# PSUM banks dealt anew in one layer of a hybrid encoder: two for projections, three for attention's scores

## The chip, the cores and the metric

The kernel runs on one core of a Trainium2 chip. The metric is the device time of one execution in microseconds (us). The median of three runs before the change is 2429.84 us (2428.33 to 2432.44).

## What is computed

One layer over 2048 prompt tokens and 64 sample tokens of width 1024, in fp32. A combined input projection feeds three mixers: a convolution with a gated linear recurrence (A), a multi-scale pooling (B) and stick-breaking attention with four heads of 64 (C). An output projection and a SwiGLU feed-forward part of width 2816 follow, each with a residual addition.

```python
def trunk_layer(x, lw, conv_buf, lru_h, pool_buf, k_past, v_past, pos0):
    h = rms_norm(x, lw["attn_norm"])
    proj = jnp.einsum("bld,de->ble", h, lw["w_in"])
    x_a, g_a, u_b, q, k, v = jnp.split(proj, SPLITS, axis=-1)
    xc, new_conv = causal_conv(x_a, conv_buf, lw["conv_w"], lw["conv_b"])
    y_lru, new_h = rg_lru(xc, lru_h, ...)
    y_a = y_lru * jax.nn.gelu(g_a, approximate=True)
    y_b, new_pool = multiscale_pool(u_b, pool_buf, pos0, lw["pool_w"], lw["pool_scale"])
    q = rms_norm(q.reshape(B, L, N_HEADS_C, HEAD_DIM), lw["q_norm"]) * (HEAD_DIM ** -0.5)
    k = rms_norm(k.reshape(B, L, N_HEADS_C, HEAD_DIM), lw["k_norm"])
    o = stick_breaking(q, k, v)      # exp(z - sum of softplus(z) over later keys), times v
    x = x + jnp.einsum("ble,ed->bld", jnp.concatenate([y_a, y_b, o]), lw["w_out"])
    h2 = rms_norm(x, lw["ffn_norm"])
    return x + (jax.nn.silu(h2 @ lw["w_gate"]) * (h2 @ lw["w_up"])) @ lw["w_down"]
```

## The kernel before

Every product is made in three matmuls (`mm3`): each operand is split into a rounded high part and a rest, and high x high, high x rest and rest x high are added up in one PSUM bank. A projection of 1024 inputs is therefore a group of 8 x 3 = 24 matmuls.

The prompt is worked in four token groups of 512 (`g` = 0 to 3); group 0 carries the 64 sample tokens along. For each group the input projections come in blocks of 128 outputs (`inproj`): A and G are the input of the recurrence and its GeLU gate, R the recurrence with its two gate products (`ps_g`, one matmul each), B and b the pooling, Q, K and V attention's inputs. Since a bank holds 512 columns, group 0's 576 tokens take two chunks of 288 (`chunks`), the others one of 512. After a Q or K projection the sums of squares of each head are made by matmuls with a selector (`ev_`), for the norm.

Attention goes over query tiles of 128 against up to 512 keys (`att_qtile`): scores in a bank z, a sigmoid by ScalarE in place, a running product (scan) by VectorE from z into `C` in SBUF, then transposes by TensorE into a bank `tp`, a split of these by ScalarE and VectorE, and products with V into the bank `av`. Then come the output projection in chunks of 256 tokens (`OUT`), whose groups are added to the residual on VectorE (L1005), the second norm, and the feed-forward part with a PSUM pool of its own.

PSUM has eight banks; until the feed-forward part they are dealt out by tag. Before: `mm` three (projections, gates, sums of squares from group 1 on, V, output projection), `tp` two, z two, `av` one. A tag's tiles go round its banks: a tile may be written when the last reader of an earlier tile in that bank is done.

```python
    def ps_mm():
        return psum.tile([P, 512], F32, name="mm", tag="mm", bufs=prm("nmm", 3))
    def ps_st(k):
        if k == 0:
            return ps_mm()
...
        if k == 2:
            return psum.tile([P, GW], F32, name="z", tag="z", bufs=prm("nz", 2))
```

The order of the work on each engine is not the program's: a planner with a timeline of its own takes at each step the ready instruction of highest priority, with the banks in view; attention has a priority of its own (`att`). The engines then work these orders strictly in turn. All numbers that steer it stand in the table `PRM`.

Of the kernel before, what the change touches and what calls it, by code (L numbers as in the profile page):

```python
# [2 lines left out]
PRM = {'accf': 2.0, 'aend': 0.0, 'alag': 15.0, 'alag0': 20.0, 'aspan': 4.0, 'att': 100.0, 'b_C': 5.0, 'b_K': 2.0, 'b_V': 2.0, 'b_aTh': 2.0, 'b_aTl': 2.0, 'b_hl': 1.0, 'b_ms': 2.0, 'b_om': 2.0, 'b_raw': 3.0, 'b_rbk': 1.0, 'b_vT': 1.0, 'b_vf': 3.0, 'b_vp': 2.0, 'b_vs': 2.0, 'b_x2': 2.0, 'b_xh': 3.0, 'b_xk': 3.0, 'b_xr': 3.0, 'b_xt': 2.0, 'cpos': 0.0, 'db': 1.0, 'ev': 0.0, 'fine': 1.0, 'ge': 0.0, 'gelb': 2.0, 'h2p': 3.0, 'lru': 100.0, 'md': 2.0, 'mhp': 0.0, 'mlast': 6.0, 'nmm': 3.0, 'nt': 100.0, 'o0': 'P0_P1_p0_G0_m0_A0_L0_R0_p1_S_l0_m1_B0_n0_A1_L1_l1_G1_R1_n1_b0_B1_A2_G2_G3_A3_R2_b1_X_Q0_Q1_R3_q0_u0_K0_q1_K1_u1_k0_k1_V_w0_w1', 'o1': 'A0_G0_A1_R0_G1_S_A2_R1_B0_G2_A3_R2_G3_B1_X_Q0_b0_R3_Q1_K0_q0_q1_u0_V_u1_K1_k0_w0_b1_k1_w1', 'o3': 'A0_G0_A1_R0_B0_G1_A2_R1_b0_G2_R2_G3_B1_A3_b1_R3', 'qlo': 1.0, 'sqb': 1.0, 'stt': 0.0, 'stt0': 2.0, 'vl': 1.0, 'vpp': 0.0, 'wd0': 1.0, 'wd1': 2.0, 'wl': 300.0, 'wm': 0.0, 'wod': 6.0, 'wok': 4.0, 'wsp': 100.0, 'xpl': 6.0, 'xrp': 0.0}  # L3
def prm(n,d):
    return type(d)(PRM.get(n,d))
# [44 lines left out]
def hybrid_layer(ctx: ExitStack, tc: tile.TileContext, x_all, x_t, w_in, w_out, w_gu, w_dn, par, gates, poolw,  # L50
# [29 lines left out]
    def mm3(out, lh, ll, rh, rl, start, stop):  # L80
        mm(out, lh, rh, start, False)
        mm(out, lh, rl, False, False)
        mm(out, ll, rh, False, stop)
# [65 lines left out]
# [6 lines that stand above are left out]
        if k == 1:  # L155
            return ps_t().rearrange('p a b -> p (a b)')
        if k == 2:
            return psum.tile([P, GW], F32, name="z", tag="z", bufs=prm("nz", 2))
        return psum.tile([P, GW], F32, name="av", tag="av", bufs=1)
# [4 lines left out]
    def ps_t():  # L164
        return psum.tile([P, 4, P], F32, name="tp", tag="tp", bufs=prm("ntp", 2))
# [48 lines left out]
    def wsplit(src, spec, on_dve=0, key=None, **ax):  # L214
        w2 = wtile()
        hi, lo = w2[:, 0, :], w2[:, 1, :]
        if key in wkept:
            with hp('wl'):
                sp.dma_start(w2.bitcast(F32), wkept[key])
        else:  # L220
            st = stage()
            with hp('wl'):
                sp.dma_start(st, src)
            with hp('wsp'):
                act.copy(hi, st)
                if on_dve:
                    dve.tensor_tensor(lo, st, hi, ALU.subtract)
                else:
                    rest(lo, hi, st)
            if key is not None:  # L230
                wkept[key] = dram.tile([P, 2, 1024], F32, name=f"wk{key[0]}_{key[1]}")
                sp.dma_start(wkept[key], w2.bitcast(F32))
        return hi.rearrange(spec, **ax), lo.rearrange(spec, **ax)
# [92 lines left out]
    def QK_parts(g, which, j):  # L326
# [3 lines left out]
        def mm_():  # L330
            raw = pq.tile([P, WM], F32, name="raw", bufs=prm("b_raw", 2))
            sq = pq.tile([P, WM], F32, name="sq", bufs=prm("b_sq", 1))
            for ps, a, b in inproj(g, which, j):
                leave(raw[:, a:b], ps[:, :b - a], g, a)
                act.activation(sq[:, a:b], raw[:, a:b] if g == 0 else ps[:, :b - a], AF.Square)
            st["raw"], st["sq"] = raw, sq
# [129 lines left out]
    def chunks(g):  # L466
        return [(0, 288), (288, 576)] if g == 0 else [(0, 512)]
# [3 lines left out]
    def inproj(g, wi, part):  # L471
        hi, lo = hT[g]
        wcnt[0] += 1
        wh, wl = wsplit(w_in[wi, :, part * 1024:(part + 1) * 1024], "p (k e) -> p k e", k=8,
                        on_dve=prm('wd0', 0) <= wcnt[0] < prm('wd1', 0), key=(wi, part))
        res = []
        for (a, b) in chunks(g):
            ps = ps_mm()
            for k in range(KD):
                mm3(ps[:, :b - a], wh[:, k, :], wl[:, k, :], hi[:, k, a:b], lo[:, k, a:b], k == 0, k == KD - 1)  # L480
            res.append((ps, a, b))
        return res
# [296 lines left out]
    def IN(g):  # L779
# [8 lines left out]
        o = "o0" if g == 0 else "o3" if g == NG - 1 else "o1"  # L788
        o = PRM[o].replace("_", " ")
        for tok in o.split():  # L790
# [121 lines left out]
    alag = prm("alag", 0.0)  # L912
# [464 lines left out]
```

## Time and profile before

| | |
|---|---|
| median of three runs | 2429.84 us |
| the profiled execution: its own time | 2430.59 us |
| its span | 2428.8 us |
| TensorE (PE) busy | 2315.6 us, 95% |
| VectorE (DVE) busy | 1561.7 us, 64% |
| GpSimd (POOL) busy | 1112.7 us, 46% |
| ScalarE (ACT) busy | 965.6 us, 40% |
| mean granted clock of TensorE | 0.975 of full speed |

A share of busy time is a mean over stages with different limits. The input projections and attention take the time to about 850 us, the output projection goes on until about 990 us, and the feed-forward part takes the rest. Waits are told as "engine, tile, line <- engine, tile, line that released it". A busy TensorE at a granted clock under 1 is busy for longer with the same work.

### The profile page before, as it was taken

The numbers are of one execution on the slowest core, as the hardware profiler recorded it, in microseconds if no ns is written. First come the engines' busy times: TensorE is split into PE (matmuls) and PEld (weight loads), VectorE is DVE, ScalarE is ACT, GpSimd is POOL, SyncE is SP. The second block draws the span as 40 slices with busy tenths as digits, with TensorE's granted clock in tenths as the row PEclk, the third lists the DMA queues.
The fourth block names the chain that finished last, engine by engine and source line by source line (L and its number), as shares of the span: only waits on it lengthen the run. The fifth ranks groups of instructions, "written<-read, shape, count | busy, mean of one in ns | idle before, by whom it ended". The sixth has DMA issues, their size and how long they took to land.

```text
span 2428.8 us, 38577 instructions
## 1 busy us (share of the span) xinstructions
PE 2315.6 (95%) x14230; PEld 2204.5 (91%) x14230; DVE 1561.7 (64%) x2514; ACT 965.6 (40%) x1804; POOL 1112.7 (46%) x818
## 2 busy tenths in 40 slices
PE   6987999999889989889999999999999999999999
PEld 6976778779678989889999999999999999999999
DVE  4568486796798644696676768655554655555455
ACT  4545364464565422233333343334333433333332
POOL 4533030131131133576565666656565765655552
PEclk8999999999999999999999999999999999999999
DMA  8986777656546354774343348633333563333332
GB/s 281 262 280 197 222 219 225 192 192 206 170 150 175 104 146 129 250 233 131 113 139 118 123 147 267 237 105 122 109 108 114 160 214 108 118 112 108 115 110 74
DMA packets 228478, 399.90 MB, mean 165 GB/s; under 512 B 37697, under 2 KB 99714, under 8 KB 220354
## 3 DMA queue, kind: packets, MB, share of 16 engines
q1 hardware_dynamic: 228290, 397.44, 52.6%
q8 instruction: 112, 1.84, 0.3%
q14 instruction: 76, 0.62, 0.1%
HBM read 300.81 MB, written 96.54 MB: 164 GB/s over the span
## 4 chain that ended last, share of the span: by engine, by line
PE 72%; DVE 12%; DMA 9%; issue 3%; ACT 2%; SPq 1%; POOL 1%; DVEq 0%; ACTq 0%; POOLq 0%
PE gu L78 33%; PE dn L78 20%; PE mm L78 14%; PE z L78 2%; PE av L78 2%; DVE C L661 1%; PE tp L705 1%; DMA rb<-xrow 1%; DMA kscr<-hl 1%; PE tp L78 1%; DVE xc L533 1%; DMA rbk<-row 1%; DMA x1all<-xr 1%; DMA wk<-w 1%; DVE al L1226 1%
## 5 line engine op out<-in xcount | busy, mean ns | idle before, releaser
L86 POOL TENSOR_TENSOR w<-x,w 128x512 fp32r<-128x512 f32 x462 | 640.7, 1401 | 509.7 <-ACT w L1103 478.4
L78 PE MATMUL dn<-ah,wd 128*128 128x352 f32 x2112 | 548.0, 324 | 5.4 <-ACT ah L1225 3.4
L78 PE MATMUL gu<-ht,w 128*128 128x352 f32 x2112 | 545.8, 323 | 7.3 <-DVE u L1180 7.1
L1103 ACT CAST w<-x 128x512 fp32r<-128x512 f32 x462 | 279.0, 619 | 521.2 <-PE gu L78 295.8
L78 PE MATMUL mm<-hTh,w 128*128 128x512 f32 (+3 forms) x1632 | 431.2, 342 | 13.7 <-DVE xr L1005 7.3
L78 PE MATMUL gu<-hb,w 128*128 128x352 f32 x1584 | 417.3, 325 | 9.0 <-DMA x<-in_w_gu 7.3
L1256 DVE TENSOR_TENSOR acc<-dn,acc 128x352 f32<-128x352 f32 x528 | 273.1, 522 | 217.5 <-PE dn L78 216.9
L78 PEld LDWEIGHTS dn<-ah,wd 128*128 128x128 f32 x2112 | 376.4, 189 | 7.6 <-ACT ah L1225 4.2
L78 PEld LDWEIGHTS gu<-ht,w 128*128 128x128 f32 x2112 | 375.1, 188 | 8.9 <-issue 5.9
L78 PE MATMUL dn<-al,wd 128*128 128x352 f32 x1056 | 342.4, 324 | 3.3 <-DVE al L1226 3.3
L78 PE MATMUL gu<-lt,w 128*128 128x352 f32 x1056 | 341.0, 323 | 0.0
L78 PEld LDWEIGHTS mm<-hTh,w 128*128 128x128 f32 x1632 | 290.2, 194 | 44.3 <-DVE xr L1005 8.5
L78 PEld LDWEIGHTS gu<-hb,w 128*128 128x128 f32 x1584 | 284.1, 189 | 11.1 <-ACT w L1103 9.5
L78 PE MATMUL mm<-hTl,w 128*128 128x512 f32 (+3 forms) x816 | 277.6, 341 | 0.8 <-DVE hTl L303 0.4
L78 PE MATMUL gu<-lb,w 128*128 128x352 f32 x792 | 257.1, 325 | 0.0
L86 POOL TENSOR_TENSOR wd<-x,wd 128x512 fp32r<-128x512 f32 x132 | 192.4, 1478 | 51.6 <-ACT wd L1244 51.6
L78 PEld LDWEIGHTS dn<-al,wd 128*128 128x128 f32 x1056 | 199.7, 189 | 4.5 <-DVE al L1226 4.5
L78 PEld LDWEIGHTS gu<-lt,w 128*128 128x128 f32 x1056 | 198.6, 188 | 0.0
L78 PEld LDWEIGHTS mm<-hTl,w 128*128 128x128 f32 x816 | 157.8, 193 | 15.7 <-issue 1.4
L661 DVE TENSOR_TENSOR_SCAN C<-z,C,zero 128x512 f32<-128x512 f32 (+4 forms) x148 | 160.6, 1087 | 13.9 <-ACT z L653 7.5
L1180 DVE TENSOR_TENSOR u<-gu,u 128x352 f32<-128x352 f32 x132 | 68.9, 522 | 129.1 <-PE gu L78 128.8
L78 PEld LDWEIGHTS gu<-lb,w 128*128 128x128 f32 x792 | 150.0, 189 | 0.0
(272 smaller groups left out, 3540.5 us busy)
## 6 DMA issues: line engine op xcount, KB each, us to landing
x<-in_w_gu SPq DMA_DIRECT2D x220, 256.0 KB, 3.3
w<-wk SPq DMA_DIRECT2D x46, 1024.0 KB, 5.7
x<-wsc SPq DMA_DIRECT2D x176, 256.0 KB, 3.4
x<-in_w_dn SPq DMA_DIRECT2D x132, 256.0 KB, 2.8
wsc<-x SPq DMA_DIRECT2D x88, 256.0 KB, 2.7
wk<-w SPq DMA_DIRECT2D x16, 1024.0 KB, 9.1
V<-vscr SPq DMA_DIRECT2D x40, 256.0 KB, 3.8
K<-kscr SPq DMA_DIRECT2D x40, 256.0 KB, 3.6
```

What stands on the lines that cost most here:

```text
L78: pe.matmul(out, lhsT, rhs, start=start, stop=stop)
L86: gp.tensor_tensor(out, src, hi, ALU.subtract)
L533: dve.scalar_tensor_tensor(xc[:, a:b], xa[:, s + j:s + j + b - a], pv("cw", c * 4 + j), xc[:, a:b], ALU.mult, ALU.add)
L661: dve.tensor_tensor_scan(C[:n, :w][:, ::-1], om[:n, :w][:, ::-1], zero1[:n].to_broadcast([n, w]), carry, ALU.mult, ALU.add)
L705: pe.transpose(tp[:, kt, :], at[:, kt * P:(kt + 1) * P], ident)
L1103: act.copy(w[:, 0, :], src)
L1180: add = lambda o, x, y: dve.tensor_tensor(o, x, y, ALU.add)
L1226: dve.tensor_tensor(al[:, cs], o, ah[:, cs], ALU.subtract)
L1256: dve.tensor_tensor(acc[:, d, a:b], ps[:, :HT], acc[:, d, a:b], ALU.add)
```

## The change

In `PRM`, `nmm` goes from 3 to 2, a new entry `nz` of 3 takes the place of the default 2, and `stt` goes from 0 to 2; `stt0` was 2 already. So `mm` has two banks and z three. `ev_` takes its bank from `ps_st(prm('stt0', 0) if g == 0 else prm('stt', 0))`: the sums of squares of groups 1 to 3 move from `mm` to z, where those of group 0 were. In `inproj`, every chunk that does not begin at column 0 takes a bank of z. Only group 0 has such a chunk: columns 288 to 575, that is 224 prompt tokens and the 64 sample tokens.

```diff
-PRM = {... 'nmm': 3.0, 'nt': 100.0, ... 'stt': 0.0, 'stt0': 2.0, ...}
+PRM = {... 'nmm': 2.0, 'nz': 3.0, 'nt': 100.0, ... 'stt': 2.0, 'stt0': 2.0, ...}
...
         for (a, b) in chunks(g):
-            ps = ps_mm()
+            ps = ps_st(2) if a else ps_mm()
             for k in range(KD):
                 mm3(ps[:, :b - a], wh[:, k, :], wl[:, k, :], hi[:, k, a:b], lo[:, k, a:b], k == 0, k == KD - 1)
             res.append((ps, a, b))
```

The planner then writes another order. Three places follow; the numbers in the names tell tiles apart, and the same number is the same tile before and after.

TensorE's order at the first Q projections of group 0: mm_674 and mm_699 (z_699 after) are the two chunks of one projection, mm_755 begins the next, and the tiles tp_475, tp_490 and tp_505 belong to V. Before:

```order
L78 MATMUL mm_674<-hTh_200,w2_667 128x288
L426 MATMUL tp_490<-ident_147,vf_487 128x128 x2
L78 MATMUL tp_475<-vf_472,dm_202 128x256
L78 MATMUL tp_475<-vf_458,em_203 128x256
L426 MATMUL tp_505<-ident_147,vf_502 128x128 x2
L78 MATMUL mm_699<-hTh_200,w2_667 128x288
```

After:

```order
L78 MATMUL z_699<-hTl_201,w2_667 128x288
L78 MATMUL z_699<-hTh_200,w2_667 128x288
L78 MATMUL tp_475<-vf_472,dm_202 128x256
L78 MATMUL tp_475<-vf_458,em_203 128x256
L426 MATMUL tp_505<-ident_147,vf_502 128x128 x2
L78 MATMUL mm_755<-hTh_200,w2_748 128x288
```

The 24 matmuls of the second chunk stand ahead of V's tiles instead of behind them, and the next projection follows these.

TensorE's order in attention of group 3: z_N are the scores of a query tile, C_(N+4) their scan, tp its transposes. The tiles' order is z_6385, 6398, 6421, 6434, 6493, 6506, 6529, 6542. Before:

```order
L78 MATMUL z_6529<-K_6487,q2_6167 128x512 x2
L78 MATMUL mm_7820<-hTh_200,w2_7785 128x256
L78 MATMUL mm_7820<-hTl_201,w2_7785 128x256
L78 MATMUL mm_7847<-hTh_200,w2_7785 128x256
L78 MATMUL mm_7847<-hTl_201,w2_7785 128x256
L78 MATMUL mm_7895<-hTh_200,w2_7785 128x256
L78 MATMUL mm_7895<-hTl_201,w2_7785 128x256
L705 MATMUL tp_6499<-ident_147,C_6497 128x128 x4
L78 MATMUL av_6174<-aTh_6419,V_6381 128x256
L78 MATMUL z_6542<-K_6487,q2_6167 128x512 x2
```

After:

```order
L78 MATMUL z_6529<-K_6487,q2_6167 128x512 x2
L78 MATMUL av_6174<-aTh_6343,V_6305 128x256
L705 MATMUL tp_6391<-ident_147,C_6389 128x128 x4
L78 MATMUL z_6542<-K_6487,q2_6167 128x512 x2
L705 MATMUL tp_6404<-ident_147,C_6402 128x128 x4
```

Behind z_6529 came the transposes of the tile two back (z_6493); now come those of the tile six back (z_6385).

TensorE's order at the gates of group 0's third block: mm_1881 to mm_1890 are the two gate products in two chunks, mm_1913 and mm_1916 the pooling product. Before:

```order
L78 MATMUL mm_1881<-xc_1578,gw_179 128x288
L78 MATMUL mm_1884<-xc_1578,gw_179 128x288
L705 MATMUL tp_1743<-ident_147,C_1741 128x128
L78 MATMUL z_1839<-K_1730,q2_1727 128x384 x2
L78 MATMUL mm_1887<-xc_1578,gw_179 128x288
L78 MATMUL mm_1890<-xc_1578,gw_179 128x288
L705 MATMUL tp_1754<-ident_147,C_1751 128x128 x2
L78 MATMUL z_1852<-K_1730,q2_1727 128x512 x2
L78 MATMUL mm_1913<-xc_1508,pw_180 128x288
L78 MATMUL mm_1916<-xc_1508,pw_180 128x288
```

After:

```order
L78 MATMUL mm_1881<-xc_1578,gw_179 128x288
L78 MATMUL mm_1884<-xc_1578,gw_179 128x288
L78 MATMUL mm_1887<-xc_1578,gw_179 128x288
L78 MATMUL mm_1890<-xc_1578,gw_179 128x288
L78 MATMUL mm_1913<-xc_1508,pw_180 128x288
L78 MATMUL mm_1916<-xc_1508,pw_180 128x288
```

Attention's rows have moved from between the six groups to behind them.

## Rows read from the trace of the kernel before

**Rows 1.** Stretches of 100 us: columns as in the first line.

```profile
core 0: us, PE busy (x) PEld busy (x) DVE busy (x) ACT busy (x) POOL busy (x), PEclk, DMA share, GB/s
...
200.00:300.00 100.00, 90.60 (x465) 76.47 (x465) 57.88 (x116) 40.62 (x80) 20.76 (x10) 0.93 0.74 219
...
700.00:800.00 100.00, 93.46 (x684) 85.64 (x683) 88.40 (x125) 60.23 (x111) 19.16 (x16) 0.98 0.57 166
...
900.00:1000.00 100.00, 85.66 (x688) 84.39 (x688) 44.21 (x82) 26.70 (x60) 38.87 (x46) 0.96 0.45 137
...
1100.00:1200.00 100.00, 100.00 (x627) 100.00 (x627) 69.05 (x113) 34.45 (x67) 59.47 (x43) 1.00 0.42 130
```

**Rows 2.** TensorE's waits, 0 to 200 us: total, times, longest.

```profile
PE mm L78 <- DVE sqt L308: 5.6, 2, 3.5
PE mm L78 <- DVE raw L308: 5.5, 1, 5.5
...
PE mm L78 <- ACT i L558: 2.5, 1, 2.5
```

**Rows 3.** TensorE's waits, 200 to 850 us.

```profile
PE z L78 <- DVE C L661: 8.4, 13, 1.9
...
PE tp L705 <- DVE C L661: 5.7, 9, 1.8
PE tp L705 <- DVE aTl L707: 3.2, 5, 1.1
PE z L78 <- ACT z L653: 2.7, 1, 2.7
```

**Rows 4.** TensorE's waits, 850 to 1100 us.

```profile
PE mm L78 <- DVE xr L1005: 7.3, 6, 2.0
```

**Rows 5.** TensorE's timeline, 126 to 142 us: start, us, operation, count, idle before.

```profile
127.12 0.42 PE L78 MATMUL mm<-hTh,w 128*128 128x288 f32 x2
...
127.52 0.43 PE L78 MATMUL mm<-hTh,w 128*128 128x288 f32 x2
...
133.38 1.33 PE L78 MATMUL mm<-xc,gw 128*128 128x288 f32 x2 [3.49 <-DVE sqt L308]
136.87 2.29 PE L78 MATMUL mm<-xc,gw 128*128 128x288 f32 x4 [2.15 <-DVE sqt L308]
```

**Rows 6.** Groups by line and shape, 0 to 1000 us: busy, mean ns, idle before.

```profile
L661 DVE TENSOR_TENSOR_SCAN C<-z,C,zero 128x512 f32<-128x512 f32 x96 | 122.2, 1275 | 13.2 <-ACT z L653 7.5 <-PE tp L705 4.8
...
L558 ACT ACTIVATE r<-mm,par_sb 128x512 f32<-128x512 f32 x12 | 8.2, 680 | 5.3 <-PE mm L78 3.0 <-issue 1.3 <-DMA mix<-r 1.0
...
L558 ACT ACTIVATE r<-mm,par_sb 128x288 f32<-128x288 f32 x8 | 4.0, 498 | 0.6 <-PE mm L78 0.6
```

**Rows 7.** Timeline of all engines, 653 to 665 us: one GeLU.

```profile
658.43 0.60 ACT L544 ACTIVATE gel<-mm 128x512 f32<-128x512 f32 x1
...
663.69 0.66 DVE L547 TENSOR_TENSOR gel<-gel,mm 128x512 f32<-128x512 f32 x1
```

**Rows 8.** TensorE's timeline, 610 to 640 us: a projection of 512 columns.

```profile
619.30 0.62 PE L78 MATMUL mm<-hTh,w 128*128 128x512 f32 x2
...
619.99 0.61 PE L78 MATMUL mm<-hTh,w 128*128 128x512 f32 x2
```

**Rows 9.** VectorE's timeline, 925 to 957 us: the output projection.

```profile
928.18 0.69 DVE L956 TENSOR_TENSOR hTl<-stg,hTh 128x512 fp32r<-128x512 f32 x1 [4.11 <-ACT hTh L954]
928.79 0.42 DVE L1005 TENSOR_TENSOR xr<-mm,xr 128x256 f32<-128x256 f32 x1
...
930.99 0.75 DVE L1005 TENSOR_TENSOR xr<-mm,xr 128x256 f32<-128x256 f32 x2
932.44 0.42 DVE L1005 TENSOR_TENSOR xr<-mm,xr 128x256 f32<-128x256 f32 x1 [0.70 <-PE mm L78]
...
935.78 0.42 DVE L1005 TENSOR_TENSOR xr<-mm,xr 128x256 f32<-128x256 f32 x1 [2.62 <-PE mm L78]
```

**Rows 10.** SP's timeline, 846 to 860 us: DMA issues.

```profile
850.55 0.34 SPq L1054 DMA_DIRECT2D xh<-x1all  x1
851.00 0.37 SPq L1013 DMA_DIRECT2D x1all<-xr  x1
```

More of the change, by code (lines that the diff above doesn't have):

```diff
@@ L2 @@
 from contextlib import contextmanager
-PRM = {'accf': 2.0, 'aend': 0.0, 'alag': 15.0, 'alag0': 20.0, 'aspan': 4.0, 'att': 100.0, 'b_C': 5.0, 'b_K': 2.0, 'b_V': 2.0, 'b_aTh': 2.0, 'b_aTl': 2.0, 'b_hl': 1.0, 'b_ms': 2.0, 'b_om': 2.0, 'b_raw': 3.0, 'b_rbk': 1.0, 'b_vT': 1.0, 'b_vf': 3.0, 'b_vp': 2.0, 'b_vs': 2.0, 'b_x2': 2.0, 'b_xh': 3.0, 'b_xk': 3.0, 'b_xr': 3.0, 'b_xt': 2.0, 'cpos': 0.0, 'db': 1.0, 'ev': 0.0, 'fine': 1.0, 'ge': 0.0, 'gelb': 2.0, 'h2p': 3.0, 'lru': 100.0, 'md': 2.0, 'mhp': 0.0, 'mlast': 6.0, 'nmm': 3.0, 'nt': 100.0, 'o0': 'P0_P1_p0_G0_m0_A0_L0_R0_p1_S_l0_m1_B0_n0_A1_L1_l1_G1_R1_n1_b0_B1_A2_G2_G3_A3_R2_b1_X_Q0_Q1_R3_q0_u0_K0_q1_K1_u1_k0_k1_V_w0_w1', 'o1': 'A0_G0_A1_R0_G1_S_A2_R1_B0_G2_A3_R2_G3_B1_X_Q0_b0_R3_Q1_K0_q0_q1_u0_V_u1_K1_k0_w0_b1_k1_w1', 'o3': 'A0_G0_A1_R0_B0_G1_A2_R1_b0_G2_R2_G3_B1_A3_b1_R3', 'qlo': 1.0, 'sqb': 1.0, 'stt': 0.0, 'stt0': 2.0, 'vl': 1.0, 'vpp': 0.0, 'wd0': 1.0, 'wd1': 2.0, 'wl': 300.0, 'wm': 0.0, 'wod': 6.0, 'wok': 4.0, 'wsp': 100.0, 'xpl': 6.0, 'xrp': 0.0}
+PRM = {'accf': 2.0, 'aend': 0.0, 'alag': 15.0, 'alag0': 20.0, 'aspan': 4.0, 'att': 100.0, 'b_C': 5.0, 'b_K': 2.0, 'b_V': 2.0, 'b_aTh': 2.0, 'b_aTl': 2.0, 'b_hl': 1.0, 'b_ms': 2.0, 'b_om': 2.0, 'b_raw': 3.0, 'b_rbk': 1.0, 'b_vT': 1.0, 'b_vf': 3.0, 'b_vp': 2.0, 'b_vs': 2.0, 'b_x2': 2.0, 'b_xh': 3.0, 'b_xk': 3.0, 'b_xr': 3.0, 'b_xt': 2.0, 'cpos': 0.0, 'db': 1.0, 'ev': 0.0, 'fine': 1.0, 'ge': 0.0, 'gelb': 2.0, 'h2p': 3.0, 'lru': 100.0, 'md': 2.0, 'mhp': 0.0, 'mlast': 6.0, 'nmm': 2.0, 'nz': 3.0, 'nt': 100.0, 'o0': 'P0_P1_p0_G0_m0_A0_L0_R0_p1_S_l0_m1_B0_n0_A1_L1_l1_G1_R1_n1_b0_B1_A2_G2_G3_A3_R2_b1_X_Q0_Q1_R3_q0_u0_K0_q1_K1_u1_k0_k1_V_w0_w1', 'o1': 'A0_G0_A1_R0_G1_S_A2_R1_B0_G2_A3_R2_G3_B1_X_Q0_b0_R3_Q1_K0_q0_q1_u0_V_u1_K1_k0_w0_b1_k1_w1', 'o3': 'A0_G0_A1_R0_B0_G1_A2_R1_b0_G2_R2_G3_B1_A3_b1_R3', 'qlo': 1.0, 'sqb': 1.0, 'stt': 2.0, 'stt0': 2.0, 'vl': 1.0, 'vpp': 0.0, 'wd0': 1.0, 'wd1': 2.0, 'wl': 300.0, 'wm': 0.0, 'wod': 6.0, 'wok': 4.0, 'wsp': 100.0, 'xpl': 6.0, 'xrp': 0.0}
 def prm(n,d):
```

## The prediction

> **What bounds the kernel now.** I read the stretches of 100 us first [rows 1]. From 1100 us on TensorE is busy all the time at full clock; that half is the feed-forward part, whose PSUM pool the change does not touch, and it stays as it is. Everything that can move lies before about 1000 us: there TensorE is busy for 91%, 93% and 86% of the stretches 200:300, 700:800 and 900:1000, and its granted clock is 0.93, 0.98 and 0.96 in them. So I read next whom TensorE waits for in that part, in three pieces. Up to 200 us it waits for VectorE to empty banks of the tag `mm` (`raw`, `sqt`: 5.5 and 5.6 us) and for ScalarE's sigmoid on a gate bank (2.5 us) [rows 2]. From 200 to 850 us attention's banks and results come first: z for the scan that still reads the bank (8.4 us in 13 waits), z for ScalarE (2.7), transposes for the scan's result (5.7 in 9) and for the bank of earlier transposes (3.2) [rows 3]. In the output projection it waits 7.3 us for the addition that empties `mm` [rows 4]. These waits add up to 41 us, 1.7% of the time: that is the field in which the banks are dealt anew. TensorE works its queue in order, so whatever stands behind a wait waits too.
>
> **The change part by part.** It removes and adds no arithmetic: the number of instructions on each engine is the same, and the bytes moved too. Banks change owner, and the planner, which writes the order with the banks in view, writes another one on all engines.
>
> *First projections.* For the first 512 tokens each projection has two groups of 24 matmuls; the second now goes to z, whose three banks are free until attention begins, so five banks serve where three did. Columns of 288 go through three in 0.40 us, 0.133 us each [rows 5], a group is 24 x 0.133 = 3.2 us. In the first place of the order above, one such group (z_699) now stands ahead of the wait for the first bank; that wait is 5.5 us [rows 2], set by the landing of `rb`, which does not move, so 3.2 us of it are filled. In the gates of the first channel block the two waits for `sqt` are 3.49 and 2.15 us [rows 5]; the first stays (the bank of the same projection), behind it now comes a group in z, and the second, 2.15 us, is covered. Gain 3.2 + 2.2 = 5.4 us; ends 0 and 11.1 (all of both waits).
>
> *Attention's third bank.* A scan of 512 columns takes 1.275 us [rows 6]. One bank more lets TensorE run one tile further before it needs the scan, so a wait up to about 1.1 us goes whole and a longer one shrinks by as much. Of the 13 + 1 waits in [rows 3] only the longest (1.9, 2.7) exceed that: 8.4 + 2.7 - 0.8 - 1.6 = 8.7 us go. But VectorE is busy for 88% of 700:800 [rows 1]; what TensorE no longer waits at z it meets partly at the next thing VectorE does, the bank of the transposes, whose 3.2 us I let grow by 2. Net gain 6.7, ends 0 and 11.1.
>
> *The distance from scores to transposes.* The second place of the order shows z two tiles ahead of the transposes before and six after. A scan then has four tiles more of time. I take two thirds of the 5.7 us [rows 3], 3.8; ends 0 and 5.7.
>
> *Two banks for the gates.* Third place of the order: six gate and pool groups follow each other with two banks between them, where three banks and attention's matmuls stood between them before. The third needs the bank of the first, whose sigmoid takes 0.50 us at 288 columns [rows 6]. What a group then waits lies between nothing, if ScalarE starts at once, and the 2.5 us that one wait on `i` took [rows 2]; I take 0.7, nearer to nothing since the sigmoid is short, four times 2.8 us. In token groups 1 to 3 a gate pair (0.68 us of sigmoid [rows 6]) takes both banks 12 times, and the projection behind it waits for the first: 0.3 us each, halved since attention's matmuls stand between in about half the places: 1.8. Loss 4.6, ends 0 and 13.6 (four times 2.5 and 3.6).
>
> *The GeLU bank.* It is held from its group's end to the last multiplication: the square starts at 658.43 and the multiplication ends at 664.35, 5.9 us [rows 7]. With two banks the group after next needs it, and the one between takes 24 x 0.23 = 5.5 us (three 512-column matmuls start within 0.69 us [rows 8]). The two are about equal: 0.4 us for each of 12, or 5 us, and somewhat more where the square starts late. As attention stands between most of them I take 1 us; ends 0 and 8.
>
> *Sums of squares.* From group 1 on they leave `mm` for z; they are two columns wide, the same matmuls as before, and hold a bank for a microsecond or so. I put this at nothing: z's third bank is the cover, and without it some 0.7 us for each of 12 is the price.
>
> *Output projection.* The additions leave VectorE in order, behind casts that wait for loads: at 928.18 the subtraction comes after 4.11 us of waiting, the addition behind it at 928.79, then two at 930.99, one at 932.44, and from there one every 2.9 us, TensorE's own pace [rows 9]. With three banks TensorE is two groups ahead in such a burst, with two banks one. The bank freed at 929.2 takes a group to 932.1; the next, 2.9 us long, ends at 935.0, where its predecessor was added at 932.44 already: one group, 2.9 us, is lost at the end of the burst. A second burst near 950 us loses 1.4 in the same way. A third, near 860, loses 2.9, but there the new order gives as much back: the load of `xh` (850.55) stood ahead of the store of `xr` (851.00) that frees the buffer SP waits for [rows 10], and now stands further ahead of both. Loss 4.3, ends 0 and 8.7.
>
> *Clock.* In 200:300 TensorE idles 9.4 us and the clock of 0.93 costs another 7; in 700:800 it is 6.5 idle and 2 [rows 1]. In these rows the part at 1.2 GHz follows the idle time at 0.3 to 0.7 us for each us. I take 0.3, for gains and losses alike.
>
> **Sum.** -5.4 - 6.7 - 3.8 + 4.6 + 1.0 + 4.3 = -6.0 us, with the clock -7.8 us. The profiled execution took 2430.6 us, 0.8 above the median of the runs; 2430.6 - 7.8 - 0.8 gives 2422.0 us.
>
> **Rivals.**
>
> *Slower: two `mm` banks become the wait.* Place: the output projection and the 12 GeLU groups. Price: three bursts of 2.9 us (8.7), 8 for GeLU, 8 for the gates, while the gains shrink by a third to 10.6: +14.1, with clock +18, 2448 us. It decides from the point where new waits on `mm` exceed 16 us, the sum of the three gains. For it speaks that evacuations of `mm` are late in [rows 7] and [rows 9] for reasons that banks do not mend; against it that the planner knew of two banks and put attention's matmuls between. Chance 0.31. The Trainium skill, "TensorE: Matmul & The Clock Gate", A second HAM failure mode, tells of a kernel in which cycling through PSUM banks let TensorE idle between groups often enough that its clock swung; the clock of 0.93 in [rows 1] agrees that short waits cost clock here, and no row shows it for two banks.
>
> *No change: the gains are given back.* VectorE at 88% sets the pace of attention, and the waits for z come back as waits for transposes; the 16 us of gains shrink to 10, which the losses take: 2429 us. For it speaks [rows 1], against it that TensorE is busy for 93% of the same stretch. Chance 0.25. The same page, HAM oscillation, reports that double-buffering PSUM brought one kernel no further gain; a third bank would do the same only if nothing waited for it, and [rows 3] has 11 us that do.
>
> *More than the sum: attention's waits go whole.* With six tiles between scores and transposes all of 11.1 + 5.7 goes, and 11.1 in the first part, the losses stay: -18, with clock -23, 2406 us. Chance 0.12; it lies on the forecast's side.
>
> **How the numbers follow.** My forecast, 2412 to 2425, has 0.32; with the larger gain faster than by 0.2% (4.9 us, about what a measurement here can tell from no change) has 0.44, within it 0.25, slower 0.31. All gains at their ends without a loss would be 27.9 x 1.3 = 36 us, all losses without a gain 13.6 + 8 + 8.7 + 0.7 x 12 = 38.7, x 1.3 = 50 us. That is 2394 to 2480; neither end is likely. For 8 in 10 I go to the time of the slower rival above and just past that of the larger gain below: 2402 to 2448.
>
> **What would show it.** Right: no z row under attention's scan among TensorE's waits from 200 to 850 us, or under 4 us of it; the wait for `raw` near 59 us down to about 2.3 us; the row for `xr` in 850:1100 at 11 to 12 us instead of 7.3; 1100 us onwards unchanged. Wrong: waits of `mm` on `gel` or `i` beyond 10 us, a new wait for K's load at the start of a token group's attention (attention now runs earlier than the projections that feed it), or a change in the feed-forward part.

## The result, and the profile after

The changed kernel takes 2461.4 us (median of four runs, 2458.6 to 2464.9) against 2429.1 us before in the same comparison: ratio 1.0132, 95% interval 1.0116 to 1.0148. The forecast was 2422 us, within 2402 to 2448. The profiled execution has a span of 2457.9 us; TensorE's mean granted clock is 0.972 instead of 0.975.

First the stretches of 100 us, as in [rows 1]:

```profile
core 0: us, PE busy (x) PEld busy (x) DVE busy (x) ACT busy (x) POOL busy (x), PEclk, DMA share, GB/s
200.00:300.00 100.00, 86.40 (x448) 72.52 (x449) 52.45 (x98) 34.97 (x73) 20.63 (x13) 0.91 0.67 199
700.00:800.00 100.00, 86.51 (x525) 71.88 (x526) 92.07 (x128) 63.17 (x111) 26.27 (x16) 0.97 0.52 151
900.00:1000.00 100.00, 89.87 (x694) 88.36 (x693) 45.19 (x77) 28.43 (x63) 36.85 (x42) 0.97 0.44 127
```

In 200:300 TensorE is busy for 86.4% instead of 90.6%, in 700:800 for 86.5% instead of 93.5%, with VectorE at 92% there.

TensorE's waits from 0 to 200 us (total, times, longest), to be held against [rows 2]:

```profile
PE mm L78 <- DVE xc L533: 8.2, 1, 8.2
PE z L78 <- ACT sq L335: 7.0, 1, 7.0
PE mm L78 <- DVE raw L308: 6.3, 1, 6.3
```

The two largest did not exist before. The first is a gate product that waits for the convolution's result, the second the sums of squares of a K block that wait for the squares. Neither waits for a bank. From 200 to 850 us, against [rows 3]:

```profile
PE z L78 <- DVE C L661: 13.9, 15, 2.0
PE tp L705 <- DVE C L661: 7.5, 4, 4.8
...
PE tp L705 <- DVE aTl L707: 6.2, 8, 1.3
...
PE mm L78 <- DVE gel L547: 3.1, 2, 2.1
```

The wait of z for the scan, which the third bank was to end, has grown from 8.4 to 13.9 us, and the one for the transposes' bank from 3.2 to 6.2. From 850 to 1100 us, against [rows 4]:

```profile
PE mm L78 <- DVE xr L1005: 12.2, 8, 3.1
```

**Where the time went.** I put both traces on one axis: TensorE's matmuls in its own order, each weighed by its columns at full clock, and for each sum of work the time from the first matmul to there. The differences to the kernel before (us, minus is ahead), for the changed kernel and four of the experiments below:

```
work done           50   100   150   200   300   500   600   725  2000
before gets there   84   155   226   295   419   657   781   929  2294
changed kernel    -5.7  -5.1  19.5  12.1  13.0  19.8  26.6  29.1  29.1
chunk_alone       -8.6 -13.1   7.7   7.7   9.8   7.0   7.1  12.1  13.5
banks_no_chunk     8.0  17.4  23.1  12.7  12.5  19.4  25.7  23.8  25.9
chunk_and_sums    -8.0 -15.3   3.0  -7.0  -8.0  -1.8   1.3   0.2  -1.0
late_x_two_hl     -8.5  -7.5   4.9  -6.5 -13.6 -16.0 -11.6 -12.3 -10.5
```

The changed kernel is 5.7 us ahead at 84 us, the size that the prediction gave its first term. Between work 100 and 150 it loses 24.7 us: the same work takes 95.8 us instead of 71.1, of which TensorE is idle for 26.2 instead of 10.4; the rest, 8.9 us, is slower work. It gets 7 back until 295 us, loses 14 in attention up to work 600, 3 more to the end of the output projection, and nothing after that. Against `chunk_and_sums`, which has the same chunks and sums but three `mm` and two z banks, it is 19 us behind at 295 us already, and 6 more up to work 600: what the dealing of the banks costs arises for the larger part at the start.

The two new waits, in TensorE's timeline (start, us, operation, count, idle before):

```profile
117.79 0.29 PE L78 MATMUL mm<-hTh,w 128*128 128x288 f32 x1
125.04 2.33 PE L78 MATMUL z<-sel,sq 128*128 128x2 f32 x10 [6.97 <-ACT sq L335]
127.30 0.61 PE L78 MATMUL z<-hTh,w 128*128 128x288 f32 x1
...
165.00 0.29 PE L78 MATMUL mm<-hTh,w 128*128 128x288 f32 x1
173.52 4.21 PE L78 MATMUL mm<-xc,gw 128*128 128x288 f32 x8 [8.23 <-DVE xc L533]
177.75 2.17 PE L78 MATMUL mm<-xc,pw 128*128 128x288 f32 x4
...
180.22 0.29 PE L78 MATMUL z<-hTh,w 128*128 128x288 f32 x1
```

Behind each stands a group of 24 matmuls in a bank of z whose inputs have long been there. Before, these two groups stood ahead of the waiting instruction: the sums of squares came at 124.31 us after 0.38 us of waiting. The order of the planner that the prediction showed for the gates (its third place) is this second wait; the prediction looked at the banks there and not at what the gates read.

Why the inputs are late shows on the engines that make them. These are the waits from 100 to 180 us of ScalarE and then of VectorE in the changed kernel, and last the same row of VectorE in the kernel before:

```profile
ACT hl L314 <- DMA qscr<-hl: 11.8, 1, 11.8
ACT hl L314 <- DMA qscr_s<-hl: 7.1, 1, 7.1
```

```profile
DVE hl L315 <- ACT hl L314: 17.2, 3, 9.5
```

```profile
DVE hl L315 <- ACT hl L314: 3.7, 3, 2.7
```

`hl` holds the split rows of a block of queries or keys on their way to DRAM, and has one buffer. The cast into it waits until the store of the rows ahead of it has landed (at 116.83 us; the cast begins at 116.85). VectorE's subtraction stands behind that cast, and behind the subtraction the work that the squares are made from. So the squares are there at 125.0 us, no earlier than before (124.3), although TensorE has come to them 6 us earlier. In `chunk_and_sums` the same group stands behind the same sums; VectorE waits 0.8 us for the cast there, and the sums begin at 119.3 us without a wait. The group's place on TensorE is thus not enough for the loss; the orders of ScalarE and VectorE that the planner wrote with two `mm` banks belong to it.

Last, the same 80 us in stretches of 20, first of the kernel before, then of the changed one:

```profile
160.00:180.00 20.00, 17.84 (x124) 16.57 (x122) 12.28 (x36) 8.72 (x19) 5.88 (x5) 1.00 0.95 348
180.00:200.00 20.00, 14.07 (x62) 10.76 (x62) 19.57 (x33) 13.93 (x29) 7.74 (x6) 0.83 0.55 154
200.00:220.00 20.00, 17.67 (x87) 14.34 (x87) 19.34 (x35) 12.63 (x23) 12.98 (x6) 1.00 0.62 179
220.00:240.00 20.00, 15.59 (x86) 13.50 (x85) 13.18 (x29) 7.12 (x16) 4.41 (x3) 0.95 0.85 276
```

```profile
160.00:180.00 20.00, 11.75 (x56) 8.75 (x55) 14.09 (x30) 8.34 (x19) 5.85 (x5) 0.74 0.83 306
180.00:200.00 20.00, 13.08 (x57) 9.89 (x56) 17.09 (x39) 11.66 (x24) 1.64 (x2) 0.66 0.50 152
200.00:220.00 20.00, 16.55 (x83) 12.65 (x83) 15.48 (x25) 8.52 (x19) 8.02 (x7) 1.00 0.70 190
220.00:240.00 20.00, 14.72 (x65) 13.04 (x66) 11.74 (x20) 9.90 (x16) 7.51 (x4) 0.66 0.61 181
```

The clock column (third from the end) is 1.00, 0.83, 1.00, 0.95 before and 0.74, 0.66, 1.00, 0.66 after: the long waits are followed by time at 1.2 GHz, so they cost more than their length (15.8 us more of idle time between work 100 and 150 came with 8.9 us more of slower work).

### The profile page after: what moved, and what is told of

Read it like the earlier page. It is cut to its first block, busy times and chain, and to the rows that moved or that the text cites. A ratio compares the mean times of both kernels' runs of the same rounds, so it can differ in the third digit from the quotient of the medians.

```text
span 2457.9 us, 38618 instructions
## 1 busy us (share of the span) xinstructions
PE 2320.8 (94%) x14230; PEld 2203.3 (90%) x14230; DVE 1553.2 (63%) x2514; ACT 964.7 (39%) x1804; POOL 1106.4 (45%) x818
## 4 chain that ended last, share of the span: by engine, by line
PE 59%; DVE 3%; DMA 3%; issue 1%; POOL 1%; SPq 0%; ACT 0%; DVEq 0%; ACTq 0%; POOLq 0%
PE gu L78 33%; PE dn L78 20%; PE mm L78 5%; DMA x1all<-xr 1%; DVE al L1226 1%; PE av L78 1%; DMA acc<-x1all 1%; DMA xh<-x1all 0%; PE tp L705 0%; PE z L78 0%; DMA x<-in_w_gu 0%; DVE s L1223 0%; DVE xh L1150 0%; DMA xg<-hsc2t 0%; DMA stg<-mix 0%
## 5 line engine op out<-in xcount | busy, mean ns | idle before, releaser
L78 PE MATMUL mm<-hTh,w 128*128 128x512 f32 (+3 forms) x1408 | 386.4, 350 | 20.9 <-DVE xr L1005 12.2
L78 PEld LDWEIGHTS mm<-hTh,w 128*128 128x128 f32 x1408 | 254.0, 195 | 52.9 <-DVE xr L1005 11.1
L78 PE MATMUL mm<-hTl,w 128*128 128x512 f32 (+3 forms) x704 | 246.6, 350 | 0.8 <-POOL hTl L303 0.8
L78 PEld LDWEIGHTS mm<-hTl,w 128*128 128x128 f32 x704 | 136.8, 194 | 17.4 <-POOL hTl L303 2.3
```

What stands on the lines that cost most here:

```text
L78: pe.matmul(out, lhsT, rhs, start=start, stop=stop)
```

## The experiments

All ratios are to the kernel before on the same chip; "us" is the ratio less one, times 2428.

```
run                       ratio (95% interval)       us   mm  z  chunk in z  sums in z
changed kernel            1.0132 (1.0116, 1.0148)   +32    2  3  yes         yes
chunk_alone               1.0054 (1.0032, 1.0075)   +13    3  2  yes         no
chunk_and_sums            1.0027 (1.0013, 1.0040)    +7    3  2  yes         yes
z_two                     1.0105 (1.0086, 1.0123)   +25    2  2  yes         yes
banks_no_chunk            1.0124 (1.0105, 1.0144)   +30    2  3  no          yes
order_mended              1.0109 (1.0090, 1.0128)   +26    2  3  yes         yes
z_three_pinned            1.0105 (1.0085, 1.0126)   +25    2  3  yes         yes
mm_three_pinned           1.0085 (1.0062, 1.0109)   +21    3  2  yes         yes
order_of_three            1.0197 (1.0174, 1.0220)   +48    2  3  yes         yes
chunk_two_hl              1.0063 (1.0040, 1.0086)   +15    3  2  yes         no
late_x_before             1.0064 (1.0048, 1.0081)   +16    3  2  no          no
late_x_chunk_sums         1.0015 (1.0001, 1.0029)    +4    3  2  yes         yes
late_x_two_hl             0.9959 (0.9943, 0.9975)   -10    3  2  yes         yes
late_x_two_hl_before      1.0060 (1.0041, 1.0078)   +15    3  2  no          no
late_x_two_hl_after       1.0038 (1.0024, 1.0051)    +9    2  3  yes         yes
light_after               1.0094 (1.0067, 1.0122)   +23    2  3  yes         yes
light_before              0.9975 (0.9960, 0.9990)    -6    3  2  no          no
out_z_after               1.0136 (1.0120, 1.0152)   +33    2  3  yes         yes
out_z_best                1.0009 (0.9997, 1.0022)    +2    3  2  yes         yes
```

### The parts of the change, one at a time

`chunk_alone` makes the first of these two edits alone, `banks_no_chunk` the second alone, `z_two` both with `nz` at 2, `chunk_and_sums` the first and, of the second, `stt`:

```diff
-            ps = ps_mm()
+            ps = ps_st(2) if a else ps_mm()
...
-PRM = {... 'nmm': 3.0, 'nt': 100.0, ... 'stt': 0.0, ...}
+PRM = {... 'nmm': 2.0, 'nz': 3.0, 'nt': 100.0, ... 'stt': 2.0, ...}
```

> Only the second chunk of group 0's projections goes to z; mm keeps three banks, z two, the sums of squares of groups 1 to 3 stay in mm. Theory A (the second chunks in z let the planner queue the sums of squares of K and the gates ahead of a free projection group, and TensorE idles behind them between 120 and 250 us): the gain of 5.7 us in the first 85 us and a loss of about 25 us from 120 to 250 us, so about 2448 us (2441 to 2455), with the waits on sq near 125 us and on xc near 173 us as in the changed kernel. Theory B (two mm banks make the loss): only the gain of the first projections, about 2423 us (2419 to 2426).

> The changed kernel with both chunks of a projection in mm again: mm two banks, z three, the sums of squares of groups 1 to 3 in z. Theory A: what is left is the creeping loss from 250 to 850 us and the 5 us of the output projection, +8 to +20 us on the kernel before, 2437 to 2449 us. Theory B: the whole loss stays or grows, 2461 us or more, as both chunks of group 0 now share two banks.

> The changed kernel with two z banks instead of three (one bank of PSUM stays empty): what the third z bank is worth by itself. If it bought what the prediction's second and third terms say (6.7 + 3.8 us, with the clock 13), this run is 10 us or more above the changed kernel, 2471 us or more. If VectorE sets the pace of attention and the bank buys next to nothing, it is within 5 us of it, 2456 to 2466 us.

> The second chunks and the sums of squares of all groups in z, with mm at three banks and z at two. The prediction put the sums of squares at nothing (0.7 us for each of 12 without the cover of a third z bank). If that holds, this run is within 3 us of the one with the chunks alone: 2439 to 2446 us. If the sums of squares in z disturb attention, it is 8 us or more above it, 2450 us or more.

Neither theory holds alone. The chunks alone took 2442.3 us, at the low end of what A said, but without its waits on sq and xc. The banks without the chunks took 2457.2, between A and B: that kernel is 17 us behind after 155 us, with both chunks of group 0 in two banks (its waits for banks of `mm` up to 200 us are 9.3 us on `raw` and 8.0 on `xa`), and level with the changed kernel from 295 us on (the table above). Two z banks took 2453.7, below both expectations, and the chunks with the sums 2434.9, below both of theirs. Step by step from the kernel before: chunks +13, sums -6, the third mm bank away +19, the third z bank +7, together +33 with rounding, against +32. So the third z bank, which was to gain 13, gains nothing and seems to cost (the two intervals touch). The sums of squares cost nothing, as the prediction said; with the intervals as they are they may even gain.

The Trainium skill ("Perfetto Trace Analysis", Matmul Optimizations) asks that all eight PSUM banks be used. Here the measurement differs: seven banks (`z_two`) took 7 us less than eight, with intervals that touch, so the eighth bank brought no gain.

What chunks alone do shows in their first 230 us. The two groups of 24 matmuls stand behind the sums of squares and the gates as in the changed kernel. TensorE is 13 us ahead at 155 us and 8 behind at 226. The longest wait in between is in the waits from 100 to 200 us of `chunk_alone` and, below it, in those from 100 to 260 us of `chunk_and_sums`:

```profile
PE z L78 <- DMA K<-kscr: 9.2, 1, 9.2
```

```profile
PE z L78 <- DMA K<-kscr: 9.8, 1, 9.8
```

It is the first score of attention, waiting for the first keys. These come through DRAM: normed, split, stored, loaded again. The first score begins at 173.8 us before and at 174.0 in `chunk_alone`.

### Bank or order

Two banks of `mm` change two things, what TensorE waits for and the order in which the planner has it work. To separate them I held TensorE's queue in an order taken from another of these kernels: every instruction is ranked by its place there, and each matmul is tied behind the one ahead of it, in issue order only. (`order_of_three` has the ranks without the ties, on all engines.)

```diff
+    def queue(self, kind):
+        last = None
+        for _, r in sorted((x for x in self.all if x[1].ins.engine == kind), key=lambda x: x[0]):
+            if last is not None:
+                self.tc.add_manual_dep(r.ins, last.ins.name, mybir.DependencyInfo(
+                    mybir.DependencyClass.NoSync, mybir.DependencyReason.DATA), reason="the queue's order")
+            last = r
```

> The changed kernel (mm two banks, z three) with TensorE's queue held, instruction for instruction, in the order that the planner wrote for two z banks; the other engines follow it. The kernel with two z banks took 2453 us, 8 less than with three. If the planner's order is what the third bank costs, this run takes 2447 to 2454 us, at most that of two banks, since at equal order a bank more can only shorten waits. If the bank itself costs time, it takes the 2461 us of the changed kernel.

> Three mm banks and two z banks, chunks and sums of squares in z, with TensorE's queue held in the order that the planner wrote for two mm and two z banks. That order took 2453 us with two mm banks; with its own order three mm banks took 2442 us (chunks alone). If the third mm bank was lost through the order, this run stays at 2449 to 2454 us; if it was lost through waits for a free bank, it comes down to 2440 to 2445 us.

> The changed kernel's banks (mm two, z three, chunks and sums in z), every instruction ranked by its place in the order that the planner wrote for three mm and two z banks; where a bank is not free in the planner's view, the next in rank goes first (994 of TensorE's 14042 instructions end more than 20 places away from that order, against 3323 in the changed kernel). If the loss of the 25 us between three mm banks and the changed kernel is a matter of the order that the planner chose, and the banks cost the 5 us by which pinned orders differed, this run takes 2434 to 2442 us. If two mm banks force the loss, 2450 to 2461 us.

Both pinned runs, 2453.9 and 2449.9 us, lie in the ranges expected if the order is the cause, the second at the edge of its range. In the traces of `z_two`, `z_three_pinned` and `mm_three_pinned` all 14230 matmuls of TensorE follow each other in the same order; of VectorE's instructions 93% or more keep their place and none moves by more than 23.

Three readings. At one and the same order, a third z bank is worth nothing (1.0105 with two and with three, within about 7 us). At one and the same order, a third mm bank is worth 5 us (1.0105 to 1.0085; the intervals overlap, so this is a size and not a proof). With the same three mm and two z banks, the order written for two mm banks takes 14 us more than their own (1.0085 against 1.0027, intervals apart). So the larger part of what the third mm bank was worth lies in the order that it allows.

Why a free bank buys nothing shows in the waits from 200 to 850 us of the two kernels with equal order, first with two z banks and three of `mm`, then with three z banks and two (in these kernels all lines read L68, that of the ranking helper):

```profile
PE tp L68 <- DVE C L68: 11.9, 16, 2.7
PE z L68 <- DVE C L68: 10.6, 16, 2.1
PE av L68 <- DVE aTl L68: 6.7, 5, 3.9
PE tp L68 <- DVE aTl L68: 3.5, 5, 1.4
```

```profile
PE tp L68 <- DVE C L68: 9.7, 15, 2.0
PE av L68 <- DVE aTl L68: 8.5, 5, 4.2
PE tp L68 <- DVE aTl L68: 7.4, 7, 2.8
```

The wait of z is gone with three z banks, 10.6 us. Of these, 5.7 come back at the next two things that VectorE does (6.7 to 8.5, 3.5 to 7.4), and the rest in other rows: all of TensorE's waits in this stretch add up to 46.1 us with two z banks and to 46.6 with three. The two kernels differ by an mm bank as well, so not all of what comes back need be the z bank's doing.

`order_of_three`, beyond both expectations at 2474.4 us, speaks against the obvious conclusion, that the planner merely chose badly. With two mm banks, the order of three, followed as far as the banks allow, costs another 16 us. The better order cannot simply be carried over to two banks; that no third order would do better is not shown. What within the order of two mm banks costs the time was tried next.

### The first 230 us

`order_mended` moves the two waiting instructions in the hand-written order (`o0`; l1 are the sums of squares, R2 the gates):

```diff
-A1_L1_l1_G1_R1
+A1_L1_G1_l1_R1
...
-A2_G2_G3_A3_R2_b1_X_Q0_Q1_R3
+A2_G2_G3_A3_b1_X_Q0_R2_Q1_R3
```

> The changed kernel with two entries of its hand-written order moved: the sums of squares of K's second block behind the whole next projection, and the gates of the third channel block behind the first Q projection. Banks as in the changed kernel. Theory A: the two waits of 7.0 us (sq, near 125 us) and 8.2 us (xc, near 173 us) go and with them some half-speed clock: 10 to 20 us below the changed kernel, 2441 to 2451 us. Theory B: the waits only move to other rows, within 5 us of the changed kernel, 2456 to 2466 us.

It took 2453.2 us, 6 off, between the two theories. TensorE's waits from 100 to 260 us say why:

```profile
PE mm L78 <- DVE xc L629: 6.5, 1, 6.5
PE z L78 <- issue: 4.9, 1, 4.9
PE tp L705 <- DVE C L657: 4.0, 1, 4.0
```

The two waits of 7.0 and 8.2 us are gone, and the next instructions wait instead: the pooling product for its input, 6.5 us, the first scores, 4.9 (their keys landed at 178.86 us, they began at 178.95). What makes the inputs late has not moved: ScalarE waits 7.5 and 9.4 us for the two stores of queries, and VectorE 15.6 us for the cast. So I asked whether the first keys set this stretch. In `chunk_two_hl` the split of queries and keys (`hl`) has two buffers instead of one; in the runs called `late_x` the loads of x that groups 2 and 3 need for their norms, 4 MB that SP issues before 120 us, stand behind the load of the first keys (`first[0]`):

```diff
-        sp.dma_start(xt[:n], src)
+        r = sp.dma_start(xt[:n], src)
+        if first:
+            tc.add_manual_dep(r.ins, first[0].ins.name, mybir.DependencyInfo(
+                mybir.DependencyClass.NoSync, mybir.DependencyReason.DATA), reason="behind the first keys")
```

> The kernel with the chunks alone, and two buffers instead of one for the split rows of queries and keys (hl). Theory C: attention of group 0 cannot begin before its first keys have come through DRAM (z_1737 at 173.8 us in the chunks-alone kernel, 173.6 us before, whatever TensorE gained until then), and what delays these keys is the single hl buffer, which two stores of the queries hold for about 9 us each until they have landed. With two buffers the first scores come before 168 us, the wait of 10.1 us on K goes, and the time is 2428 to 2436 us. Rival: the DMA queues as a whole are the limit in this stretch (busy 80 to 95%), the keys land at the same time, 2440 to 2445 us.

> The kernel before, with one thing held back: the loads of x for the sums of squares of token groups 2 and 3 (8 loads of 512 KB, which SP issues in the first 120 us) stand in SP's queue behind the load of the first keys. Theory D: the DMA queues, busy 84 to 95% until 180 us, set when the first keys land and with them the start of attention (first scores near 173.6 us). Then the first scores come 5 us or more earlier and the time is 2416 to 2426 us. If something else sets that point, the first scores stay within 2 us and the time at 2426 to 2432 us.

> The same hold on the loads of x, in the kernel with chunks and sums in z and three mm banks (2435 us, first scores 171.5 us, 15 us ahead of the kernel before at equal TensorE work at 155 us and level with it at 226 us). Theory D: the lead survives the start of attention, 2415 to 2427 us. Otherwise 2431 to 2440 us.

> As the run before, with two hl buffers. By themselves two hl buffers brought the store of the first keys from 167.6 to 151.4 us, and nothing in the time, since SP issued the load of these keys at 168 us all the same. Theory D: with the queues relieved the earlier store counts, first scores before 160 us and 2410 to 2425 us. Otherwise 2431 to 2445 us.

Theory C fell: the store of the first keys came 16 us earlier, SP issued their load at 168.7 us all the same, and the time did not move. In the kernel before, theory D was right about the first scores, which came at 161.2 instead of 173.8 us, and wrong about the time: it took 16 us longer. The planner wrote another order on all engines with the hold; what in it costs the time is not shown. The hold on the kernel with chunks and sums gave 2431.1 us, at the edge of no effect. With both edits together that kernel took 2418.9 us, in the range that D gave, with first scores at 161.6 us. But not by D's mechanism: its lead does not outlast the start of attention. It is 7.5 us ahead at 155 us and 4.9 behind at 226, much as without the edits, and at 295 us both are ahead by 6.5 to 7. It draws away after that, to 16 us at 657, where the kernel without the edits has 1.8 left; which of the two edits does this there, and how, is not shown. SP's timeline there (its lines are five further down) has the load of the first keys at 147.65 us, in the kernel before at 169.87:

```profile
147.65 0.43 SPq L690 DMA_DIRECT2D K<-kscr  x1
```

```profile
169.87 0.97 SPq L685 DMA_DIRECT2D K<-kscr  x2
```

That version is faster than both kernels, ratio 0.9959. Each edit of it without the others is no gain: the hold alone +16, two buffers with the chunks +15, hold and buffers without the chunks +15, chunks and sums without them +7. Two more runs ask what the banks do in that company:

> The kernel before (banks and chunks as before) with the loads of x for groups 2 and 3 held behind the first keys and two hl buffers: the version of 2419 us without the chunks and sums in z. If the two edits alone make that gain, 2415 to 2424 us; if the second chunk in z is needed for it, 2430 to 2446 us (the hold alone gave 2445 us).

> The changed kernel with the same two edits: against the version of 2419 us it differs by the third mm bank given to z alone. If the loss by that bank (25 us between the same pair without the two edits) is a property of two mm banks, this run takes 2438 to 2450 us; if it came from the crowded start, 2419 to 2430 us.

The loss by the banks is there again: 0.9959 with three mm and two z banks, 1.0038 with two and three, 19 us. Without the two edits the same pair was 25 us apart. It comes with these banks, and not with the crowded start alone. In the changed kernel the two edits gain 23 us: VectorE's wait for the cast into `hl` is down to 0.7 us from 100 to 180 us, and at 295 us the kernel is 1 us ahead of the kernel before instead of 12 behind. This agrees with the stores as the cause of the late inputs; the two edits were not tried there one at a time.

### Is it VectorE?

In the changed kernel VectorE is busy for 92% of 700:800, so I took some of its work away in attention, with TensorE's queue pinned:

```diff
-                        dve.tensor_tensor(aTl[:, :nk, qq * P:(qq + 1) * P], tp[:, :nk, :],
-                                          aTh[:, :nk, qq * P:(qq + 1) * P], ALU.subtract)
+                        nl = nk // 2 if c < g else nk
+                        dve.tensor_tensor(aTl[:, :nl, qq * P:(qq + 1) * P], tp[:, :nl, :],
+                                          aTh[:, :nl, qq * P:(qq + 1) * P], ALU.subtract)
...
-                        mm(o, V[:, kt, :], aTl[:, kt, q0:], False, c == 0 and kt == nkt - 1 and pr == 1)
+                        mm(o, V[:, kt, :], (aTh if c < g and kt > 1 else aTl)[:, kt, q0:], False, c == 0 and kt == nkt - 1 and pr == 1)
```

> The changed kernel with TensorE's queue pinned to its own order and less VectorE work in attention: for keys of earlier token groups the rest of the weights (aTl) is made for half of the columns only, and the products of the other half read the high part in its place (left out: those rests, some 96 subtractions of 512 columns become 256 wide, about 0.3 us less each, 29 us of VectorE's work between 200 and 850 us; TensorE's work is the same). Theory E (VectorE's work comes in bunches in which it sets the pace): 12 to 20 us below the changed kernel, 2441 to 2449 us. Theory F (banks of mm or the order's gaps on TensorE set the pace, VectorE does not): at most 6 us below, 2455 to 2461 us.

> The kernel before with the same lighter VectorE work and TensorE's queue pinned to its own order. Theory E: VectorE binds less there, so the same relief gives at most half of what it gives the changed kernel: 2420 to 2425 us. Theory F: as much in both kernels, whatever that is.

The changed kernel gained 9 us and the kernel before 6. Theory E wanted 12 to 20 and at most half of it before; theory F at most 6, and the same in both. The gap between the kernels closes from 32 to 29 us. VectorE seems to have a price in both, and the difference between them hardly to be its doing; the pair is inconclusive, since the intervals are 7 and 13 us wide, and no run pins the queue without the lighter work. In 680 to 785 us the relief did not even show in VectorE's share in the changed kernel, as other work moved in (changed kernel, then `light_after`), while it fell from 97.05 to 89.79 us in the kernel before:

```profile
680.00:785.00 105.00, 89.93 (x502) 71.11 (x501) 97.88 (x134) 68.97 (x116) 24.67 (x14) 0.97 0.47 140
```

```profile
680.00:785.00 105.00, 91.99 (x563) 76.47 (x562) 97.21 (x144) 71.12 (x122) 25.81 (x15) 1.00 0.50 151
```

### The output projection

```diff
-            ps = ps_mm()
+            ps = ps_st(2) if d % 2 else ps_mm()
```

> The changed kernel with every second group of the output projection in a z bank, so five banks instead of two. If the wait on xr is for a free bank, as the prediction says, its 12.2 us go to 5 us or less and the time is 4 to 9 us below the changed kernel, 2452 to 2457 us. If VectorE's lateness sets it in any case, within 3 us of it, 2458 to 2464 us.

> The version of 2419 us (three mm banks, two z, chunks and sums of squares in z, loads of x held behind the first keys, two hl buffers) with every second group of the output projection in a z bank. Its wait on xr is 9.3 us with three banks; if it is for a bank, 3 to 7 us of it go: 2412 to 2417 us. Otherwise 2417 to 2422 us.

TensorE's waits from 840 to 1100 us in `out_z_after`:

```profile
PE tp L78 <- DVE ss L1022: 9.0, 1, 9.0
PE gu L78 <- ACT w L1103: 8.1, 3, 6.9
PE gu L78 <- DVE u L1180: 5.7, 1, 5.7
```

The wait on `xr`, 12.2 us, is gone, as it should be if it was for a bank, as the prediction said. The time is the same. The planner wrote another order again, in which less of the output projection stands among attention's last tiles: ahead of the last scores come 120 of its 1536 matmuls, where the changed kernel has 230. Between work 575 and 625 `out_z_after` loses 7 us on the changed kernel, gains 12 by work 700, and loses 5 again by 725, where the sums for the second norm wait 9.0 us. In the faster version the same edit cost 12 us; there the count falls from 435 to 144, and the same stretch loses 14 us. The second expectation failed in the same manner as the prediction: it priced the wait that goes and not the order that comes.

## Why the prediction was wrong

*First projections, -5.4.* The size, 5.7 us ahead at 84 us, is right by luck. The wait on `raw` near 59 us was to fall to 2.3 us; it is 6.3, one group later. The group in z fills another wait, that of V's tiles for `vT` (3.0 to 0.6 us), and the rest is clock: from 5 to 84 us TensorE is busy for 64 us in both kernels, but at 0.89 instead of 0.83 of full speed. As a term of a sum it failed. What TensorE gains there it loses by 230 us to inputs that it reaches earlier than they are ready, in the changed kernel at the sums of squares and the gates, in `chunk_alone` at the first keys. The prediction never asked what stood at the end of that stage.

*Attention's third bank, -6.7, and the distance to the transposes, -3.8.* Wrong. At equal order the waits of z go as computed, 10.6 us, and the time stays the same; with its own order the bank brings no gain. The step that failed is "what TensorE no longer waits at z it meets partly", put at 2 us: measured, more than half of it is met again in two rows, and what is left buys nothing. The two terms are also not independent. Between a tile's scores and its transposes stood 2.0 further tiles of scores on average before, and 4.2 in the changed kernel, so the order was read rightly; but scores that run so far ahead use up the bank, and z waits 13.9 us for scans again. The rival "no change" had the reason.

*Two banks for the gates, +4.6, and the GeLU bank, +1.* Small, and not split as the prediction had it: waits for a gate bank come to 2.0 us (`r` 0.8, `i` 1.2) instead of 2.5, and those on `gel` to 3.1 instead of 0.4. The third mm bank at equal order is worth some 5 us. What had no term is the other 14 us of the 19: the order that the planner writes for two banks. This is the largest error of the sum. The prediction did show the third place of the order and read the absence of attention's matmuls as a loss of cover of 0.7 us a group; the gates themselves waited 8.2 us for their input from VectorE.

*Sums of squares, 0.* Right for their banks (+13 to +7 when they move, not a loss). Another matter is the wait of 7.0 us at 125 us, which is theirs: it comes from late squares, not from a bank.

*Output projection, +4.3.* Right: the waits on `xr` went from 7.3 to 12.2 us, and the stage lost 3 us at equal work.

*Clock, 0.3 us for each us.* Too low where it counted. Between work 100 and 150 TensorE idles 15.8 us more and the stage loses 24.7, so 0.56 us for each.

*Sum and rivals.* Of -6.0 us of terms, those that were gains (-15.9) brought nothing that lasted, those that were losses (+9.9) came to some 7 us of waits, and some 14 us for the order, with its clock, were missing. The slower rival, 2448 us, had the sign and the tag `mm`, but its place was wrong: it expected the waits on `mm` banks, and those that it named came to 15 us in all, 5 more than before on `xr`. Its price was short because it, too, counted banks. Unchanged from 1100 us on was right: the difference is 29.8 us at 1110 us and 29.1 at 2294.

What stays open is which feature of the orders for two mm banks costs the time. At the start it is late inputs, as shown above. Between 295 and 780 us the changed kernel loses 14 us on the kernel before, but `chunk_and_sums` loses 8 there too; the lighter work on VectorE does not close the gap, and no single wait explains it. One feature tells the orders apart that the planner wrote itself: with three mm banks 427 to 459 of the output projection's 1536 matmuls stand ahead of attention's last scores, with two 230 to 290, and 257 in the pinned order, which lost its 14 us to the order alone. The two runs with the output projection in z, 230 to 120 and 435 to 144, lost 7 and 14 us in that stretch. But `order_of_three` has 431 with two mm banks and is the slowest of all, and no run changed this feature alone, so it is a lead and not a cause.

## What to carry to other kernels

Where a planner writes the order with the banks in view, a bank is worth what it does to the order, and the waits in the trace price only the smaller part: here 5 us of 19. Before crediting a wait that goes, name the instruction that waits next on the same engine, and before crediting a stage, find the input that its successor needs and when that arrives; a lead that ends at a late input is worth nothing. Follow a late input back through the engines that make it: here the first long wait of TensorE began with a store to DRAM that held a single buffer. To bring one such input forward need not help either, as the first keys showed. To tell bank from order, hold one engine's queue in a fixed order and change the banks alone.

## What the runs showed of the hardware

These rows show how much of a wait is paid a second time, as slower work behind it. Behind the 8.23 us at 173.5 us the changed kernel's stretches of 4 us read:

```profile
172.00:176.00 4.00, 2.48 (x5) 1.68 (x6) 2.57 (x8) 1.53 (x4) 0.00 (x0) 0.50 1.03 413
176.00:180.00 4.00, 3.98 (x11) 2.01 (x10) 2.03 (x3) 3.20 (x7) 1.12 (x1) 0.55 0.19 60
180.00:184.00 4.00, 3.57 (x27) 3.34 (x26) 1.80 (x2) 3.31 (x4) 0.42 (x1) 1.00 0.22 74
```

TensorE works again from 173.5 us on and is granted 1.2 GHz until about 180: the twelve products of that time took 4.21 and 2.17 us, 0.53 us each. In the kernel before, at full clock, two of the same kind took 0.65 us, and two behind the wait of 3.49 us 1.33 [rows 5]:

```profile
129.25 0.65 PE L78 MATMUL mm<-xc,gw 128*128 128x288 f32 x2
```

Over the whole stage from work 100 to 150, 15.8 us more of idle time went with 8.9 us more of slower work, 0.56 us for each; the prediction had taken 0.3.
